# Strassen-style down projection: another order of the seven products, and the residual added in sixteen pieces

## The chip, the cores and the metric

The kernel runs on one core of a Trainium2 chip. The metric is the device time of one execution in microseconds; the time given for a kernel is the median of several runs. The engines are named as the profile names them: PE multiplies matrices (PEld loads its weights), DVE and ACT work on vectors, POOL is used here for some vector work and to issue DMAs that add to what they find, and SP issues the plain DMAs.

## The reference

One decoder layer over 1024 prompt tokens and 64 sample tokens. The change lies in one line of it, the down projection of the gated MLP and the addition to the residual stream, and touches the start of what follows:

```python
def conv_ffn(n, prev, lw):
    a = n @ lw['ffn_w_gate']
    c = n @ lw['ffn_w_up']
    ...
    y = (jax.nn.silu(conv) * c) @ lw['ffn_w_down']        # (1024 x 2816) @ (2816 x 1024)
    ...
    y, conv_new = conv_ffn(rmsnorm(h, lw['g_ffn']), conv_prev, lw)
    h = h + y
    h = h + (p.astype(h.dtype) @ lw['ple_w_proj']) * jax.nn.sigmoid(rmsnorm(h, lw['g_ple']) @ lw['ple_w_gate'])
```

All data are float32. To keep the precision, each operand of a matmul is split into a high and a low part, and three matmuls (high by high, high by low, low by high) stand for one.

## The kernel before

**The stage.** The gated activations have been written to DRAM, one tensor `ds` for each of 22 chunks of 128 of the inner dimension; the residual `h` of the prompt lies in DRAM as `dhp`. The down projection treats the prompt rows as two halves (tiles 0 to 3 and 4 to 7), the 1024 output columns as two halves, and the inner dimension as two halves, and computes the 2x2 block product with seven products of half-size blocks in place of eight. Product numbers 1 to 7 are those of the tuple `SEVEN`. Each product has 11 steps `k`, one for each pair of inner chunks, so there are 77 steps in a fixed order (`steps`). One step on PE is 12 matmuls (`summed`, through `mm3`): four row tiles by three.

**What a step needs.** `load(p, k)` issues two DMAs of 256 KB on SP, four steps ahead in program order (product 5 has a third); they land in one of five buffers called `raw2`. For product 1 they land in `st2`, one buffer for each `k` that stays through the stage and is updated in place by products 5 and 6. `operands(p, k)`, two steps ahead, forms sums or differences with `st2` on DVE (two of 512 columns for products 5 and 6, one of 1024 for product 7, one of 512 for products 4 and 3, none for products 1 and 2), then splits: ACT casts the high part, DVE subtracts to get the low part, both into one of four buffers `o`. So a `raw2` buffer comes free for the next load when DVE has made the low part of its step, and an `o` buffer when PE has done its step. The instruction order on each engine is set by the tile framework's own scheduler, which may place an operation earlier or later than the program text has it; each engine then runs its list in order.

**What a product leaves.** A product's four PSUM accumulators are folded into `h` in SBUF at its last step (`folded(p, t)`, for each row tile `t`): products 1 and 5 by an ACT copy, the others by a DVE addition. Quadrant `h11` is rows 0 to 3 and columns 0 to 511, `h12` the same rows and the other columns, `h21` and `h22` the same for rows 4 to 7. Sums between quadrants that need no accumulator are in `folded_on`, in the steps of the product that follows. `residue(i, j)` adds the residual to a quadrant, by one 1 MB DMA from POOL that accumulates into `h`. Before, the order is 1, 5, 6, 7, 4, 3, 2, so rows 4 to 7 are finished first, by product 4 and the DMA into `h21` after it. In the steps of product 2 stand their normalisation (`normalised`: two ACT squares with a row sum, called `junk`; two small POOL operations, `ss` and `rs`; then `xs`, on DVE or on ACT and POOL) and transposition (`turned`); the scheduler starts the normalisation earlier, in product 3. The last stage (`ple_unit`) takes the rows in the order 4 to 7, then 0 to 3.

Of the kernel before, what the change touches and what calls it, by code (L numbers as in the profile page):

```python
# [13 lines left out]
ALU = mybir.AluOpType  # L14
# [4 lines left out]
P = 128  # L19
D = 1024  # L20
T = 1024
NT = 8
# [7 lines left out]
PLAN = ([0], [], [1, 2, 3])  # L30
VIAP = 20
GS0 = 1
VIAQ = 40
NWB = 10
NF = DFF // P
EPS = 1e-6
# [9 lines left out]
def step_kernel(ctx: ExitStack, tc: tile.TileContext, A):  # L46
    nc = tc.nc
    pe, act, dve, pool, sp = nc.tensor, nc.scalar, nc.vector, nc.gpsimd, nc.sync
# [1311 lines left out]
    cs = cache_stream()  # L1360
# [108 lines left out]
    def xnorm(t, xn, eng):  # L1469
        rows = P if t < NT else R  # L1470
        x = hrows(t)
        r = z["rs"][:rows, t:t + 1]
        if eng is dve:
            dve.scalar_tensor_tensor(xn[:rows], x, r, z["gb"][:rows], ALU.mult, ALU.mult)
# [109 lines left out]
    dhp, dhs = dram.tile([T, D], F32, name="dhp"), dram.tile([R, D], F32, name="dhs")  # L1584
# [290 lines left out]
    NK = NF // 2  # L1875
    opened("hp")
    residual(z["hp"])
    h, hs = z["h"], z["hs"]
# [12 lines left out]
    def xrooms(t):  # L1891

        for e in range(2):
            n = (t + 4) % NT * 2 + e
# [34 lines left out]
    def place_of(k):  # L1929
        return f"st{(k + 3) % NK}"  # L1930

    def load(p, k):
        if p == 1:
            st[k] = z["xs"].tile([P, 2, 512], F32, tag=place_of(k), name="st2", bufs=1)
        r = st[k] if p == 1 else raws()
        a, b = SOURCES[p]
        sp.dma_start(r[:, 0], rows_of(*a, k))
# [26 lines left out]
    def banks(n):  # L1964

        kinds = (pm, pm, p2t, p2t) if n % 2 else (pd, pd, pd, p2)
        return [b([P, 512], "ps_dn") for b in kinds]

    def summed(p, k, t):
        o, tt = opd[p, k], slice(t * P, t * P + P)  # L1970
        mm3(acc[p][t], o[:, 0, 0, tt], o[:, 1, 0, tt], o[:, 0, 1], o[:, 1, 1], k == 0, k == NK - 1)

    def residue(i, j):

        rows, cs = slice(i * 512, i * 512 + 512), slice(j * 512, j * 512 + 512)
        pool.dma_start(h[:, 4 * i:4 * i + 4, cs], dhp[rows, cs].rearrange("(t p) c -> p t c", p=P), accum_op=ALU.add)

    def folded(p, t):

        ps = acc[p][t]  # L1980
        h11, h12, h21, h22 = (h[:, i, j:j + 512] for i in (t, t + 4) for j in (0, 512))
        if p == 1:
            act.copy(h11, ps)
        elif p == 5:
            act.copy(h22, ps)
        elif p == 6:
            dve.tensor_tensor(h12, h11, ps, ALU.add)
        elif p == 7:
            dve.tensor_tensor(h21, h12, ps, ALU.subtract)
        else:  # L1990
            hx = {4: h21, 3: h12, 2: h11}[p]
            dve.tensor_tensor(hx, hx, ps, ALU.add)

    def folded_on(p, t):

        h12, h21, h22 = h[:, t, 512:], h[:, t + 4, 0:512], h[:, t + 4, 512:]
        if p == 7:
            dve.tensor_tensor(h12, h12, h22, ALU.add)
            dve.tensor_tensor(h22, h22, h21, ALU.add)

    def ple_gate(c):
# [41 lines left out]
    for i, (p, k) in enumerate(steps):  # L2043
        if i + 4 < len(steps):
            load(*steps[i + 4])
        if i + 2 < len(steps):
            operands(*steps[i + 2])
        if k == 0:
            acc[p] = banks(i // NK)
        q = SEVEN[i // NK - 1] if i >= NK else 0  # L2050
        if p == 2 and k == NK - 2:
            continue
        for t in range(4):
            for k_ in ((k - 1, k) if p == 2 and k == NK - 1 else (k,)):
                summed(p, k_, t)
            if k == NK - 1:
                folded(p, t)
        if q and 1 <= k <= 4:
            folded_on(q, k - 1)
        for when, quad in (((7, 3), (0, 0)), ((4, 6), (1, 1)), ((4, 7), (0, 1)), ((3, 1), (1, 0))):  # L2060
            if (p, k) == when:
                residue(*quad)
        if p == 1 and k == 1:
            for half in range(2):
                fold_sample(acc_s[half], half)
        elif p == 1 and k == 4:
            xn[NT] = normalised(NT)
        elif p == 1 and k == 7:
            turned(NT, xn[NT])
        elif p == 3 and k == 8:  # L2070
            wpl = ple_gate(0)
        elif p == 2:
            if k in (0, 1, 3, 5):
                t = 4 + (k + 1) // 2
                xn[t] = normalised(t)
            if k in (2, 4, 6, 8):
                t = 3 + k // 2
                turned(t, xn[t])
            if k in (5, 7):
                pT.append(ple_in(k // 7))  # L2080
    for t in range(2):
        xn[t] = normalised(t)


# [17 lines left out]
    def ple_proj(c):  # L2102
        return wload(z["pl"], A["ple_w_proj"][0][:, c * 256:(c + 1) * 256], 2, 256, "wj", 2, st=stg)
# [43 lines left out]
    for c in range(4):  # L2147
        last = c == 3
        nxt = None
        for n, ts in enumerate(((4, 5), (6, 7), None, (0, 1)) + (((2,), (3,)) if last else ((2, 3),))):  # L2150
            if ts:
                ple_unit(c, ts, ws)
            else:
                ple_sample(c, ws)
            if c == 0 and n < 2:
                for t in (2 * n, 2 * n + 1):
# [56 lines left out]
```

## Time and profile before

| | |
|---|---|
| median of 3 runs | 2242.73 us (2241.42 to 2244.2) |
| the profiled execution | 2243.74 us, span 2242.0 us |
| busy in the span | PE 95%, DVE 75%, ACT 61%, POOL 55% |
| first and last start of the stage's matmuls | 1871.7 and 2106.4 us |
| mean granted clock of PE over the span | 0.984 |

Times inside the execution are counted from the start of the span. In a row of the timeline stand the start, the length, the engine, the line and operation, the tile written and read, and in brackets how long the engine was idle before it and what ended that. In a row that groups instructions, three numbers with strokes are the shortest, median and longest duration in ns. In a row by stretches, each engine has its busy time and, in brackets, its instruction count. In the DMA parts, q1 is the queue of SP and q0 that of POOL.

### The profile page before, as it was taken

The page shows a single profiled execution, that of the slowest core. Times are in us where ns is not written, and L with a number is a line of the kernel's source. Part 1 is how long each engine was busy: PE and PEld are TensorE (multiplying, and loading weights), DVE is VectorE, ACT ScalarE, POOL GpSimd, SP SyncE. Part 2 cuts the span into 40 slices and gives each one's busy share as a digit, 9 for nine tenths or more (in the row PEclk, how much of TensorE's full clock was granted, in tenths as well). Part 3 has the DMA queues.
Part 4 walks back from the last instruction along what each step waited for, and adds up shares of the span by engine and source line. Part 5 has one row for each costly group of instructions (what it writes and reads, how often), then busy time and mean ns, then how long its engine had stood idle before and what let it go on. Part 6 is the DMA issues. An engine that isn't in the chain of part 4 may idle for free.

```text
span 2242.0 us, 38332 instructions
## 1 busy us (share of the span) xinstructions
PE 2140.5 (95%) x13459; PEld 1932.5 (86%) x13459; DVE 1674.3 (75%) x2542; ACT 1360.7 (61%) x3692; POOL 1232.3 (55%) x1320
## 2 busy tenths in 40 slices
PE   7999989999999999999999988999999999998999
PEld 6889978878888888887888877999999998876899
DVE  4775766467788888886878888888888877976632
ACT  5576766777778898887777765434333334434521
POOL 5675667576777777776545558665656560002000
PEclk9899999999999999999999998999999999999999
DMA  5343235413242222212422132323232327667321
GB/s 179 108 144 104 82 115 160 130 56 86 85 126 66 60 60 69 63 56 72 138 78 74 55 117 63 108 90 100 89 100 85 104 72 243 228 173 217 99 77 37
DMA packets 204354, 233.59 MB, mean 104 GB/s; under 512 B 42238, under 2 KB 146147, under 8 KB 204163
## 3 DMA queue, kind: packets, MB, share of 16 engines
q1 hardware_dynamic: 188387, 180.01, 25.6%
q0 software_dynamic: 14544, 46.67, 7.2%
q10 hardware_dynamic: 1232, 4.46, 0.5%
q8 instruction: 108, 1.77, 0.3%
q14 instruction: 83, 0.68, 0.1%
HBM read 188.52 MB, written 42.52 MB: 103 GB/s over the span
## 4 chain that ended last, share of the span: by engine, by line
PE 76%; DVE 8%; ACT 5%; DMA 5%; POOL 3%; issue 2%; SPq 0%; ACTq 0%; DVEq 0%; POOLq 0%
PE ps_gu L140 7%; PE ps_gu L141 7%; PE ps_gu L139 7%; PE ks L139 5%; PE ks L141 4%; PE ks L140 4%; PE cpv L645 2%; PE ctp L522 2%; PE ps_dn L140 2%; PE ps_dn L141 2%; PE ps_dn L139 2%; PE ps_pj L139 2%; PE ps_lt L278 2%; PE ps_pj L140 1%; PE ps_pj L141 1%
## 5 line engine op out<-in xcount | busy, mean ns | idle before, releaser
L560 ACT ACTIVATE csq<-ks 128x256 f32<-128x256 f32 x1040 | 392.5, 400 | 86.7 <-PE ks L141 77.6
L565 DVE TENSOR_REDUCE css<-csq 128x16 f32<-128x1024 f32 (+1 forms) x264 | 315.6, 1196 | 64.6 <-ACT csq L560 63.5
L116 ACT CAST wh<-st 128x512 fp32r<-128x512 f32 x176 | 108.3, 619 | 184.9 <-PE ps_gu L140 164.3
L139 PE MATMUL ks<-mv0h,cTh 128*128 128x320 f32 (+1 forms) x520 | 171.5, 332 | 6.5 <-ACT csq L560 2.9
L139 PE MATMUL ks<-mv1h,cTh 128*128 128x320 f32 (+1 forms) x520 | 169.0, 327 | 7.7 <-ACT sn L562 3.6
L604 POOL TENSOR_TENSOR chl<-craw,chl 128x1024 fp32r<-128x1024 f32 x64 | 141.3, 2207 | 57.2 <-ACT chl L603 56.6
L140 PE MATMUL ks<-mv0l,cTh 128*128 128x320 f32 (+1 forms) x520 | 152.7, 295 | 0.0
L140 PE MATMUL ks<-mv1l,cTh 128*128 128x320 f32 (+1 forms) x520 | 152.6, 295 | 0.0
L141 PE MATMUL ks<-mv0h,cTl 128*128 128x320 f32 (+1 forms) x520 | 148.3, 298 | 0.9 <-DVE cTl L117 0.8
L141 PE MATMUL ks<-mv1h,cTl 128*128 128x320 f32 (+1 forms) x520 | 148.2, 299 | 0.1
L630 POOL TENSOR_TENSOR phl<-sn,phl 128x512 fp32r<-128x512 f32 (+1 forms) x64 | 84.9, 1327 | 106.5 <-ACT phl L629 106.0
L117 DVE TENSOR_TENSOR wl<-st,wh 128x512 fp32r<-128x512 f32 x132 | 119.0, 903 | 28.4 <-ACT wh L116 28.4
L140 PE MATMUL ps_dn<-o 128*128 128x512 f32 x308 | 122.9, 399 | 8.8 <-DVE o L117 8.6
L117 POOL TENSOR_TENSOR wl<-st,wh 128x512 fp32r<-128x512 f32 x44 | 69.5, 1581 | 105.0 <-ACT wh L116 105.0
L141 PE MATMUL ps_dn<-o 128*128 128x512 f32 x308 | 121.2, 394 | 0.0
L117 DVE TENSOR_TENSOR cTl<-ctp,cTh 128x512 fp32r<-128x512 f32 (+1 forms) x136 | 90.0, 662 | 38.9 <-ACT cTh L116 38.0
L562 ACT COPY sn<-ks 128x64 f32<-128x64 f32 x520 | 116.6, 224 | 0.0
L139 PEld LDWEIGHTS ks<-mv0h,cTh 128*128 128x128 f32 x520 | 98.6, 190 | 20.6 <-ACT sn L562 7.3
L139 PEld LDWEIGHTS ks<-mv1h,cTh 128*128 128x128 f32 x520 | 98.5, 189 | 19.7 <-ACT sn L562 7.5
L139 PE MATMUL ps_dn<-o 128*128 128x512 f32 x308 | 109.9, 395 | 5.5 <-ACT o L116 5.5
L1317 POOL TENSOR_TENSOR pl<-p,ph 128x512 fp32r<-128x512 f32 (+1 forms) x96 | 97.4, 1019 | 31.3 <-DVE ph L1316 21.3
L141 PE MATMUL ps_gu<-xrh,wl 128*128 128x320 f32 x352 | 108.7, 309 | 0.0
(674 smaller groups left out, 7881.1 us busy)
## 6 DMA issues: line engine op xcount, KB each, us to landing
raw<-ds SPq DMA_DIRECT2D x77, 256.0 KB
raw<-ffn_w_down SPq DMA_DIRECT2D x66, 256.0 KB
stage<-w_in SPq DMA_DIRECT2D x48, 256.0 KB
st<-ffn_w_gate SPq DMA_DIRECT2D x44, 256.0 KB
st<-ffn_w_up SPq DMA_DIRECT2D x44, 256.0 KB
wr<-ffn_w_down SPq DMA_DIRECT2D x44, 256.0 KB
ds<-cv SPq DMA_DIRECT2D x21, 512.0 KB
oraw<-doT SPq DMA_DIRECT2D x16, 256.0 KB
```

Of the source, the lines that this page charges most:

```text
L116: act.copy(hi, src)
L117: (lo_eng or dve).tensor_tensor(lo, src, hi.bitcast(F32), ALU.subtract)
L139: pe.matmul(ps, ah, bh, start=first, stop=False)
L140: pe.matmul(ps, ah, bl, start=False, stop=False)
L141: return pe.matmul(ps, al, bh, start=False, stop=last)
L278: pe.matmul(ps, x, w, start=first, stop=last)
L560: act.activation(sq[:, f * 256:f * 256 + 256], ks[:, 0:256], AF.Square)
L562: act.copy(o.sn[:, g0 + i, :], ks[:, 256:320])
L565: dve.tensor_reduce(o.ss[:, g0 + i + 1 - n:g0 + i + 1, :].rearrange("p i h -> p (i h)"), sq2[:, :n].rearrange("p i (h n) -> p (i h) n", n= ...
L604: pool.tensor_tensor(ch[:, c0:c1, 128:256], src, ch[:, c0:c1, 0:128].bitcast(F32), ALU.subtract)
L630: pool.tensor_tensor(phl[:, :nt, 64:128], sb, phl[:, :nt, 0:64].bitcast(F32), ALU.subtract)
L1317: pool.tensor_tensor(pl[:, c0:], p[:, c0:], ph[:, c0:].bitcast(F32), ALU.subtract)
```

## The change

The order of the products becomes 1, 5, 6, 3, 7, 2, 4. Rows 0 to 3 are now finished first (by product 2), so the normalisation and transposition written in the steps of the last product now take rows 0 to 3 and stand in product 4, and the last stage takes rows 0 to 3 first; the mask `VIAQ` and the rooms for the transposed rows are mirrored with it. Product 5 is copied to `h22` and also to `h12` (four more ACT copies), product 6 goes into `h21`, and `h12` gets it through `folded_on`. The number of DVE additions is the same, 28. They are written at steps 1, 3, 5 and 7 of the following product, where they stood at steps 1 to 4. The residual comes by row tile: sixteen DMAs of 256 KB, each written two steps after the one before, the quadrants in the order 22, 11, 12, 21 in the steps of products 6, 3, 7 and 2.

```diff
-    SEVEN = (1, 5, 6, 7, 4, 3, 2)
+    SEVEN = (1, 5, 6, 3, 7, 2, 4)
...
-    def residue(i, j):
-        rows, cs = slice(i * 512, i * 512 + 512), slice(j * 512, j * 512 + 512)
-        pool.dma_start(h[:, 4 * i:4 * i + 4, cs], dhp[rows, cs].rearrange("(t p) c -> p t c", p=P), accum_op=ALU.add)
+    def residue(i, j, t):
+        rows, cs = slice((4 * i + t) * P, (4 * i + t + 1) * P), slice(j * 512, j * 512 + 512)
+        pool.dma_start(h[:, 4 * i + t, cs], dhp[rows, cs], accum_op=ALU.add)
...
         elif p == 5:
             act.copy(h22, ps)
+            act.copy(h12, ps)
         elif p == 6:
-            dve.tensor_tensor(h12, h11, ps, ALU.add)
+            dve.tensor_tensor(h21, h11, ps, ALU.add)
         elif p == 7:
-            dve.tensor_tensor(h21, h12, ps, ALU.subtract)
+            dve.tensor_tensor(h21, h21, ps, ALU.subtract)
         else:
-            hx = {4: h21, 3: h12, 2: h11}[p]
+            hx = {3: h12, 2: h11, 4: h21}[p]
             dve.tensor_tensor(hx, hx, ps, ALU.add)
...
-        if p == 7:
-            dve.tensor_tensor(h12, h12, h22, ALU.add)
+        if p == 6:
+            dve.tensor_tensor(h12, h12, h21, ALU.add)
+        elif p == 7:
             dve.tensor_tensor(h22, h22, h21, ALU.add)
...
-        if q and 1 <= k <= 4:
-            folded_on(q, k - 1)
-        for when, quad in (((7, 3), (0, 0)), ((4, 6), (1, 1)), ((4, 7), (0, 1)), ((3, 1), (1, 0))):
-            if (p, k) == when:
-                residue(*quad)
+        if q and k in (1, 3, 5, 7):
+            folded_on(q, k // 2)
+        for p0, k0, i_, j_ in ((6, 2, 1, 1), (3, 3, 0, 0), (7, 3, 0, 1), (2, 3, 1, 0)):
+            if p == p0 and k >= k0 and (k - k0) % 2 == 0 and k - k0 < 8:
+                residue(i_, j_, (k - k0) // 2)
...
-        elif p == 2:
+        elif p == 4:
             if k in (0, 1, 3, 5):
-                t = 4 + (k + 1) // 2
+                t = (k + 1) // 2
                 xn[t] = normalised(t)
```

What the scheduler makes of it is seen at three places.

ACT, where the normalisation of the first finished rows meets the casts of the operands. Before, this is in product 3: the first row casts its step 5, the cast after the first `junk` its step 6.

```order
L116 CAST o_25503<-raw2_25460 128x1024
L1465 ACTIVATE junk_25695,ss_24233<-h_24231 128x512
L116 CAST o_25522<-raw2_25480 128x1024
L1465 ACTIVATE junk_25697,ss_24233<-h_24231 128x512
L1465 ACTIVATE junk_25721,ss_24233<-h_24231 128x512
L1465 ACTIVATE junk_25723,ss_24233<-h_24231 128x512
L116 CAST o_25541<-raw2_25499 128x1024
L1465 ACTIVATE junk_25782,ss_24233<-h_24231 128x512
L1476 ACTIVATE xs_25727<-h_24231,rs_24234 128x1024
```

After, it is in product 4; the first row casts step 2, the cast after two `junk` step 3.

```order
L116 CAST o_25684<-raw2_25637 128x1024
L1465 ACTIVATE junk_25703,ss_24233<-h_24231 128x512
L1465 ACTIVATE junk_25705,ss_24233<-h_24231 128x512
L116 CAST o_25715<-raw2_25657 128x1024
L1465 ACTIVATE junk_25730,ss_24233<-h_24231 128x512
L1465 ACTIVATE junk_25732,ss_24233<-h_24231 128x512
L1465 ACTIVATE junk_25793,ss_24233<-h_24231 128x512
L116 CAST o_25743<-raw2_25680 128x1024
L1465 ACTIVATE junk_25795,ss_24233<-h_24231 128x512
L1476 ACTIVATE xs_25736<-h_24231,rs_24234 128x1024
```

Before, the first square reads a row tile of `h21`, which the last 1 MB DMA writes. After, it reads `h11`, which DVE has just finished with product 2; the DMAs into `h11` and `h12` belong to products 3 and 7.

DVE, after a product that is followed by sums between quadrants. Before, this is product 4, steps 2 and 3 (`o` is the low part of the operands, L1957 forms the operands of a later step, L1989 folds product 7, L1998 and L1999 are the sums without an accumulator):

```order
L1989 TENSOR_TENSOR h_24231<-h_24231,ps_dn_25000 128x512
L1998 TENSOR_TENSOR h_24231<-h_24231 128x512
L1989 TENSOR_TENSOR h_24231<-h_24231,ps_dn_25001 128x512
L1957 TENSOR_TENSOR raw2_25254<-raw2_25254,st2_24323 128x512
L1989 TENSOR_TENSOR h_24231<-h_24231,ps_dn_25002 128x512
L1998 TENSOR_TENSOR h_24231<-h_24231 128x512
L117 TENSOR_TENSOR o_25237<-raw2_25187,o_25237 128x1024
L1999 TENSOR_TENSOR h_24231<-h_24231 128x512
L1998 TENSOR_TENSOR h_24231<-h_24231 128x512
L1957 TENSOR_TENSOR raw2_25275<-raw2_25275,st2_24341 128x512
L1998 TENSOR_TENSOR h_24231<-h_24231 128x512
L1999 TENSOR_TENSOR h_24231<-h_24231 128x512
```

After, the same product 7 is followed by product 2 (L1990 folds product 7, L2001 is the sum that follows):

```order
L1990 TENSOR_TENSOR h_24231<-h_24231,ps_dn_25232 128x512
L117 TENSOR_TENSOR o_25447<-raw2_25403,o_25447 128x1024
L1990 TENSOR_TENSOR h_24231<-h_24231,ps_dn_25233 128x512
L2001 TENSOR_TENSOR h_24231<-h_24231 128x512
L1990 TENSOR_TENSOR h_24231<-h_24231,ps_dn_25234 128x512
L1990 TENSOR_TENSOR h_24231<-h_24231,ps_dn_25235 128x512
L2001 TENSOR_TENSOR h_24231<-h_24231 128x512
L117 TENSOR_TENSOR o_25469<-raw2_25422,o_25469 128x1024
L2001 TENSOR_TENSOR h_24231<-h_24231 128x512 x2
L117 TENSOR_TENSOR o_25488<-raw2_25444,o_25488 128x1024
```

Four sums fewer stand between the splits, and no operand is formed there. The sums are not at every other step, as the text has them, but close together again.

DVE, early in product 6. Before, the low part of step 3 (`o_24795`) comes right after the last operands of product 6:

```order
L1952 TENSOR_TENSOR st2_24403<-raw2_24890,st2_24403 128x512
L117 TENSOR_TENSOR o_24795<-st2_24264,o_24795 128x1024
L1955 TENSOR_TENSOR raw2_24910<-raw2_24910,st2_24255 128x1024
L117 TENSOR_TENSOR o_24815<-st2_24275,o_24815 128x1024
L1955 TENSOR_TENSOR raw2_24930<-raw2_24930,st2_24258 128x1024
L117 TENSOR_TENSOR o_24835<-st2_24297,o_24835 128x1024
```

After, the operands of the first two steps of product 3 stand ahead of that low part (`o_24799`):

```order
L1952 TENSOR_TENSOR st2_24403<-raw2_24896,st2_24403 128x512
L1959 TENSOR_TENSOR raw2_24917<-raw2_24917,st2_24255 128x512
L1959 TENSOR_TENSOR raw2_24937<-raw2_24937,st2_24258 128x512
L117 TENSOR_TENSOR o_24799<-st2_24264,o_24799 128x1024
L117 TENSOR_TENSOR o_24819<-st2_24275,o_24819 128x1024
L117 TENSOR_TENSOR o_24840<-st2_24297,o_24840 128x1024
```

Two loads of product 3 must now have landed before that low part is made.

On POOL the sixteen DMAs stand where the four stood, in one piece, ahead of the small operations of the normalisation. By what each waits for, the first four (`h22`) can go as soon as ACT has copied product 5, the next four (`h11`) as DVE folds product 6, the next (`h12`) as DVE folds product 3, and the last (`h21`) as DVE makes the sums of L2001.

More of the change, by code (lines that the diff above doesn't have):

```diff
@@ L32 @@
 GS0 = 1
-VIAQ = 40
+VIAQ = 130
 NWB = 10
@@ L1893, in xrooms @@
         for e in range(2):
-            n = (t + 4) % NT * 2 + e
+            n = t * 2 + e
             if n < NK:
@@ L2050, in step_kernel @@
         q = SEVEN[i // NK - 1] if i >= NK else 0
-        if p == 2 and k == NK - 2:
+        if p == 4 and k == NK - 2:
             continue
         for t in range(4):
-            for k_ in ((k - 1, k) if p == 2 and k == NK - 1 else (k,)):
+            for k_ in ((k - 1, k) if p == 4 and k == NK - 1 else (k,)):
                 summed(p, k_, t)
@@ L2069, in step_kernel @@
             turned(NT, xn[NT])
-        elif p == 3 and k == 8:
+        elif p == 2 and k == 8:
             wpl = ple_gate(0)
-        elif p == 2:
+        elif p == 4:
             if k in (0, 1, 3, 5):
-                t = 4 + (k + 1) // 2
+                t = (k + 1) // 2
                 xn[t] = normalised(t)
             if k in (2, 4, 6, 8):
-                t = 3 + k // 2
+                t = k // 2 - 1
                 turned(t, xn[t])
@@ L2080, in step_kernel @@
                 pT.append(ple_in(k // 7))
-    for t in range(2):
+    for t in (4, 5):
         xn[t] = normalised(t)
@@ L2149, in step_kernel @@
         nxt = None
-        for n, ts in enumerate(((4, 5), (6, 7), None, (0, 1)) + (((2,), (3,)) if last else ((2, 3),))):
+        for n, ts in enumerate(((0, 1), (2, 3), None, (4, 5)) + (((6,), (7,)) if last else ((6, 7),))):
             if ts:
@@ L2155, in step_kernel @@
             if c == 0 and n < 2:
-                for t in (2 * n, 2 * n + 1):
+                for t in (4 + 2 * n, 5 + 2 * n):
                     turned(t, xn[t])
```

## The prediction

> **What bounds the kernel now.** The page first: PE is the busiest engine by far, so time is won where PE waits.
>
> ```profile
> span 2242.0 us, 38332 instructions
> PE 2140.5 (95%) x13459; PEld 1932.5 (86%) x13459; DVE 1674.3 (75%) x2542; ACT 1360.7 (61%) x3692; POOL 1232.3 (55%) x1320
> ```
>
> Second, PE's timeline gives its pace with everything ready. Two starts of the same matmul, one step of 12 apart, are 2.72 us apart: 0.227 us each, 29.9 us for a product of 11 steps.
>
> ```profile
> 2046.35 0.39 PE L139 MATMUL ps_dn<-o 128*128 128x512 f32 x1
> 2049.07 0.39 PE L139 MATMUL ps_dn<-o 128*128 128x512 f32 x1
> ```
>
> Third, the stage cut at its products, all instructions counted. The rows are products 7, 4, 3 and 2; the columns are the stretch, its length, the engines' busy times, the granted clock, the DMA share and GB/s.
>
> ```profile
> 1965.00:1996.00 31.00, 29.62 (x129) 23.71 (x128) 20.43 (x21) 10.78 (x11) 1.41 (x1) 1.00 0.68 186
> 1996.00:2032.00 36.00, 31.73 (x134) 24.38 (x132) 25.74 (x33) 10.88 (x11) 2.56 (x2) 1.00 0.79 215
> 2032.00:2073.00 41.00, 34.01 (x132) 26.02 (x132) 25.67 (x28) 18.00 (x29) 13.81 (x10) 0.92 0.63 183
> 2073.00:2106.80 33.80, 33.80 (x165) 27.98 (x164) 20.62 (x25) 15.41 (x26) 1.27 (x4) 1.00 0.28 96
> ```
>
> Less 29.9 us each, the losses are 1.1, 6.1 and 11.1 us: 18.3 in three products. Product 2 has some 31 transposes among its matmuls, which account for its 3.9 us, and PE was never idle there. So 18.3 us is all that the change can win in this stretch.
>
> Fourth, who makes PE wait: the waits of PE, the four residual DMAs on POOL, and ACT and PE after the last of them.
>
> ```profile
> PE ps_dn L140 <- DVE o L117: 8.1, 8, 1.7
> PE ps_dn L139 <- ACT o L116: 4.4, 1, 4.4
> ...
> 1968.37 1.41 POOL L1976 DMA_DIRECT2D h<-dhp  x1 [91.68 <-DMA raw<-ffn_w_down]
> 2009.24 1.29 POOL L1976 DMA_DIRECT2D h<-dhp  x1 [39.47 <-DVE h L1998]
> 2013.31 1.28 POOL L1976 DMA_DIRECT2D h<-dhp  x1 [2.78 <-DVE h L1999]
> 2040.74 1.28 POOL L1976 DMA_DIRECT2D h<-dhp  x1 [26.16 <-DVE h L1992]
> ...
> 2052.56 0.63 ACT L1465 ACTIVATE junk<-h 128x512 bf16<-128x512 f32 x1 [12.86 <-DMA h<-dhp]
> 2053.19 1.03 ACT L116 CAST o<-raw 128x1024 fp32r<-128x1024 f32 x1
> ...
> 2054.27 0.80 PE L139 MATMUL ps_dn<-o 128*128 128x512 f32 x1 [4.36 <-ACT o L116]
> 2065.09 0.49 PE L140 MATMUL ps_dn<-o 128*128 128x512 f32 x1 [1.51 <-DVE o L117]
> ```
>
> ACT ran into a square that needs the last residual DMA and stood 12.86 us, with the casts of the operands queued behind it; PE used up what was prepared and stopped. That is product 3. Product 4 is another matter: two 1 MB DMAs within 4 us, and the loads of the operands beside them. The chain of waits shows a load at its usual 3.0 us (1996.27), and the same kind of load beside the residual:
>
> ```profile
> 1971.63 9.19 DMA raw<-ffn_w_down
> 1996.27 3.01 DMA raw<-ffn_w_down
> 2014.78 11.94 DMA raw<-ds
> 2040.74 11.73 DMA h<-dhp
> ```
>
> DVE's timeline says why a late load stops PE: operands of a later step stand ahead of a split that PE needs sooner, and DVE runs in order.
>
> ```profile
> 1980.93 1.23 DVE L1955 TENSOR_TENSOR raw<-raw,st 128x1024 f32<-128x1024 f32 x1 [2.05 <-DMA raw<-ffn_w_down]
> 1982.08 1.22 DVE L117 TENSOR_TENSOR o<-raw,o 128x1024 fp32r<-128x1024 f32 x1
> 2019.86 0.69 DVE L1957 TENSOR_TENSOR raw<-raw,st 128x512 f32<-128x512 f32 x1 [3.97 <-DMA raw<-ffn_w_down]
> 2020.47 1.22 DVE L117 TENSOR_TENSOR o<-raw,o 128x1024 fp32r<-128x1024 f32 x1
> ```
>
> **The change, part by part.**
>
> *The wait on the last residual goes.* In the new order the squares that start early read `h11` and `h12`. Their residual belongs to the end of products 6 and 3, a product or more earlier. The last residual (`h21`) is read again only by the fold of product 4, at the stage's end. Product 3's 11.1 us are this wait: the idle 4.36 us, the matmuls after it at half pace (granted clock 0.92 over the stretch), the idle 1.51 us, and small ones. I take back all 11.1.
>
> *The normalisation now meets product 4.* Its casts have no DMA to wait for, but DVE still forms operands there, where product 2 had none: 11 of 0.69 us, and 1.22 us of split each, 21 us of DVE in 30, beside the rows below.
>
> ```profile
> L1465 ACT ACTIVATE junk<-h x32: 617/631/637, 1310.2 to 2108.5; 128x512 bf16<-128x512 f32 x32
> L1474 DVE SCALAR_TENSOR_TENSOR xs<-h,rs,gb x6: 1272/1284/1285, 2056.9 to 2124.8; 128x1024 f32<-128x1024 f32 x6
> L1985 ACT COPY h<-ps_dn x4: 588/600/621, 1933.8 to 1935.3; 128x512 f32<-128x512 f32 x4
> ```
>
> In the new list the first `xs` stands on DVE ahead of the split of step 3. Its chain from the fold is two squares (1.3 us), the two POOL operations and `xs` itself (1.3). The POOL pair:
>
> ```profile
> 2056.91 1.91 POOL L1466 TENSOR_SCALAR ss<-ss 128x1 f32<-128x1 f32 x1
> 2058.91 1.39 POOL L1467 TENSOR_TENSOR rs<-ss,mhalf 128x1 f32<-128x1 f32 x1
> ```
>
> That is up to 3.4 us more, 6 in all. When product 2 ends, three steps are split ahead, 8.2 us of PE, so the split of step 3, 1.2 us after `xs`, comes in time. I take 1 us of loss, with 0 and 6 as ends: the 6 is one whole chain in the open.
>
> *The residual as four groups.* What each waits for sets when it goes. `h11` goes as product 6 is folded, as before (1968.4, now a few us sooner and by row tile). Before, this group cost product 7 1.1 us; now product 3 stands there, with an operand of 0.69 us in place of 1.22. I keep 1. `h12` goes as product 3 is folded, alone, in product 7. Before, this place (product 4) had 2 MB and twelve folds and sums; now there are 1 MB and four folds. Its price lies between 1.1, one group with splits three steps ahead, and 6.1, two groups and the sums; the splits will not be fully ahead, since a load is tied to the split two places before it, and product 7 has the long operands. I take 3. `h21` goes in product 2, which forms no operands on DVE, so that a late load stops no split but its own, and five buffers of loads lie ahead. I take 0.5, ends 0 and 1.1.
>
> `h22` goes at the end of product 5, about 1935 to 1940. There the queues are full until 1943.5 and then empty for 14 us:
>
> ```profile
> DMA  9997897898892899930000000000000000000006
> GB/s 346 366 382 276 271 365 192 322 358 276 292 339 85 295 290 333 336 137 5 0 0 0 0 0 0 0 0 0 0 0 0 22 0 0 0 0 0 0 0 216
> ```
>
> (1930 to 1960 in 40 parts.) The megabyte is pushed into the empty part. The DMA's own work is no larger than before: 26.0% of 25 us, 6.5 us of all 16 engines, for 1.05 MB.
>
> ```profile
> q1 hardware_dynamic: 2008, 3.65, 44.7%
> q0 software_dynamic: 528, 1.05, 26.0%
> ```
>
> (1960 to 1985; packets, MB, share.) What may hurt is DVE's list: two operands of product 3 now stand ahead of the split of step 3 of product 6. The rows of the same places before, SP's loads and the split:
>
> ```profile
> 1932.25 0.33 SPq L1937 DMA_DIRECT2D raw<-ds  x1
> 1933.46 0.33 SPq L1937 DMA_DIRECT2D raw<-ds  x1
> ...
> 1939.83 1.22 DVE L117 TENSOR_TENSOR o<-st,o 128x1024 fp32r<-128x1024 f32 x1
> ```
>
> The pair's loads are issued before the residual. The split ended at 1941.05, and PE needed it eight steps before product 6 ended at 1965, at 1943.2: 2.2 us to spare. Two operands of 0.69 us in front of it use 1.4 of them. I take 0.5 us of loss, ends 0 and 4 (the pair's loads some 4 us late).
>
> *The copies and the sums.* Four ACT copies of 0.60 us are 2.4 us at the end of product 5, where ACT waits for PE between casts (26.1 of 55 us busy) and DVE is the one that is late; nothing, and up to 1 us without that cover. Sixteen issues in place of four: each took 1.28 to 1.41 us on POOL, whole megabytes; sixteen are at most 23 us over 100, on an engine that is otherwise idle there. Nothing. The twelve folds and sums that stood together become eight and eight; their gain is within the 3 us of product 7. The last stage does the same work in the mirrored order of rows: nothing, within 1 us.
>
> ```profile
> 1905.00:1960.00 55.00, 55.00 (x245) 45.53 (x244) 50.77 (x63) 26.14 (x29) 0.00 (x0) 1.00 0.67 229
> ```
>
> **The sum.** Losses before 18.3. After: 0.5 (product 6), 1 (product 3), 3 (product 7), 0.5 (product 2), 1 (product 4), together 6. The gain is 12.3 us. The profiled execution took 2243.74 us, 1.7 more than its span and 1.0 more than the median of the runs; against the median of 2242.73 the gain leaves 2230.4.
>
> **The rivals.**
>
> *A: the lead is not rebuilt, and the change is slower.* The place is product 4: three chains of normalisation stand on DVE ahead of splits. If product 2 ends with nothing split ahead, each chain is open: 3 times 6 us is 18. With product 7 at its full 6.1 and 1.5 in products 6 and 3, that is 25.6, 7 more than now: 2250. It decides at some 5 us of PE idle a chain. For it: DVE has 21 us of operands and splits in this product. Against: product 2 has only splits on DVE, 13 of 30 us with some folds, so it can run ahead as far as the four `o` buffers allow. 0.07.
>
> *B: bursts decide, not the wait.* Each group of 1 MB stops DVE as 2 MB did before, 6.1 us in products 3, 7 and 2 of the new order, since the scheduler has put each group into one piece: with 0.5 and 1 that is 19.8, and the time is 2244, no change. For it: loads took 9.2 and 11.9 us beside a residual. Against: the first group before cost only 1.1. 0.06.
>
> *C: a fixed price for each DMA.* A plain load of 256 KB took 3.0 us; if the sixteen do the same one after the other, a group holds the queues 12 us, where 1 MB took 11.7. That is no loss by these rows, but if a group also keeps the loads back for its four completions (3.0 each on top of 11.7), three groups in operand-forming products each cost 3 to 4 us more: 2241. 0.04. The Trainium skill, DMA: Bandwidth & Descriptors, section on the anatomy of one DMA, gives about 2.0 us for each DMA plus its bytes at 436 GB/s; by this rule sixteen of them take an estimated 24 us more than four, against the change. The trace does not agree on the time of a megabyte (11.7 us, where the rule has 4.4), and the landing is nobody's wait in the new order.
>
> *D: nothing is left.* Groups spread over row tiles cost nothing, only product 4's 1 us: 2225. 0.15.
>
> **How the numbers follow.** The forecast, 2230 with its own range of 2226 to 2237, has 0.68. D has 0.15, B and C 0.10, A 0.07. A measurement of this kernel tells 0.2%, 4.5 us, from no change. Faster by that: the forecast, D and a little of C, 0.84; same, 0.08; slower 0.08. The range for 8 in 10 takes in D's 2225 and reaches to 2239, where product 7 and product 4 both take their upper ends.
>
> **What would show it.** ACT's squares should have no wait on `h<-dhp`; product 4 in the old list, now product 7, should lose about 3 us; PE's clock should be 1.00 in every product; four clusters of POOL issues near 1935, 1965, 1997 and 2028. It is wrong if PE waits on DVE in the last product by more than 6 us, or if the split of step 3 of product 6 comes late.

## The result, and the profile after

The changed kernel took 2228.22 us (median of 4 runs, 2226.04 to 2231.13), the kernel before 2242.53 beside it (4 runs, 2241.42 to 2244.2): ratio 0.9936, 95% interval 0.9919 to 0.9954, which is 14.3 us saved where 12.3 were forecast. Run again in a later session (e8 below), where the kernel before took 2245.59, it gave 0.9925 (0.9912 to 0.9938). The kernel before itself took 2242.5 to 2246.7 us in the different sessions, so below only ratios to the kernel before of the same session, or lengths inside a trace, are compared.

The page after the change, its span and engines:

```profile
span 2224.2 us, 38364 instructions
PE 2135.0 (96%) x13459; PEld 1932.2 (87%) x13459; DVE 1672.1 (75%) x2542; ACT 1361.3 (61%) x3696; POOL 1236.5 (56%) x1332
```

The work is the same; PE is busy 5.5 us less; 4.1 of that are old product 3's matmuls, partly at half pace (34.01 us busy of a usual 29.9). The stage cut at its products (6, 3, 7, 2 and 4; columns as in the prediction):

```profile
1932.40:1962.60 30.20, 30.20 (x135) 25.01 (x134) 23.54 (x28) 15.37 (x19) 4.47 (x5) 1.00 0.57 158
1962.60:1992.50 29.90, 29.90 (x134) 24.75 (x133) 23.93 (x27) 11.61 (x11) 2.62 (x3) 1.00 0.71 210
1992.50:2024.90 32.40, 30.99 (x134) 24.68 (x133) 24.99 (x25) 11.57 (x11) 3.48 (x4) 1.00 0.77 226
2024.90:2054.80 29.90, 29.90 (x133) 24.76 (x133) 19.01 (x22) 11.61 (x11) 3.48 (x4) 1.00 0.75 213
2054.80:2088.50 33.70, 33.34 (x159) 27.08 (x158) 26.88 (x31) 21.00 (x41) 11.91 (x13) 1.00 0.29 94
```

Products 6, 3 and 2 have no idle PE at all; the granted clock is 1.00 throughout. Product 7 takes 2.5 us more than 29.9, and product 4 has 25 transposes among its matmuls. What PE still waits for, from 1930 to 2090 us, is shown as the total, the number of times and the longest (1.8 us in all, 12.5 before):

```profile
PE ps_dn L140 <- DVE o L117: 1.4, 3, 0.7
PE pt L132 <- DVE xg L117: 0.4, 1, 0.4
```

The residual DMAs on POOL's timeline:

```profile
1933.27 3.80 POOL L1976 DMA_DIRECT2D h<-dhp  x4 [59.61 <-DMA raw<-ds]
1961.70 0.86 POOL L1976 DMA_DIRECT2D h<-dhp  x1 [24.63 <-DVE h L1988]
...
1995.46 0.86 POOL L1976 DMA_DIRECT2D h<-dhp  x1 [28.48 <-DVE h L1993]
1997.19 1.75 POOL L1976 DMA_DIRECT2D h<-dhp  x2 [0.87 <-DVE h L1993]
1999.52 0.86 POOL L1976 DMA_DIRECT2D h<-dhp  x1 [0.57 <-DVE h L1993]
2026.21 0.86 POOL L1976 DMA_DIRECT2D h<-dhp  x1 [25.83 <-DVE h L2001]
```

Each of the last three groups starts with the first row tile that is ready and follows the others (1995.46 to 1999.52 in the group of `h12`), where a 1 MB DMA had to wait for the fourth. ACT's first square no longer waits for a DMA, only for the fold, and nothing runs short behind it:

```profile
2056.73 0.63 ACT L1465 ACTIVATE junk<-h 128x512 bf16<-128x512 f32 x1 [3.50 <-DVE h L1993]
```

What is left of the old trouble is product 7, where 1 MB still lies among the loads (DVE, then PE):

```profile
2002.30 1.23 DVE L1955 TENSOR_TENSOR raw<-raw,st 128x1024 f32<-128x1024 f32 x1 [1.93 <-DMA raw<-ffn_w_down]
...
2008.09 1.23 DVE L1955 TENSOR_TENSOR raw<-raw,st 128x1024 f32<-128x1024 f32 x1 [2.29 <-DMA raw<-ffn_w_down]
```

```profile
2004.71 0.50 PE L140 MATMUL ps_dn<-o 128*128 128x512 f32 x1 [0.75 <-DVE o L117]
2010.50 0.50 PE L140 MATMUL ps_dn<-o 128*128 128x512 f32 x1 [0.28 <-DVE o L117]
2013.90 0.50 PE L140 MATMUL ps_dn<-o 128*128 128x512 f32 x1 [0.38 <-DVE o L117]
```

### The profile page after: what moved, and what is told of

Same layout as the page of the kernel before. It is cut to its first block, busy times and chain, and to the rows that moved or that the text cites. A ratio compares the mean times of both kernels' runs of the same rounds, so it can differ in the third digit from the quotient of the medians.

```text
span 2224.2 us, 38364 instructions
## 1 busy us (share of the span) xinstructions
PE 2135.0 (96%) x13459; PEld 1932.2 (87%) x13459; DVE 1672.1 (75%) x2542; ACT 1361.3 (61%) x3696; POOL 1236.5 (56%) x1332
## 4 chain that ended last, share of the span: by engine, by line
PE 74%; DVE 9%; DMA 5%; ACT 5%; POOL 4%; issue 3%; SPq 0%; DVEq 0%; POOLq 0%; ACTq 0%
PE ps_gu L140 7%; PE ps_gu L141 7%; PE ps_gu L139 7%; PE ks L139 5%; PE ks L141 4%; PE ks L140 4%; PE cpv L645 2%; PE ctp L522 2%; PE ps_dn L140 2%; PE ps_dn L141 2%; PE ps_dn L139 2%; PE ps_lt L278 2%; PE ps_pj L139 2%; PE ps_pj L140 1%; PE ps_pj L141 1%
## 5 line engine op out<-in xcount | busy, mean ns | idle before, releaser
L139 PE MATMUL ps_gu<-xrh,wh 128*128 128x320 f32 x352 | 108.6, 309 | 0.9 <-ACT xrh L116 0.9
```

Source lines behind the costliest of these rows:

```text
L139: pe.matmul(ps, ah, bh, start=first, stop=False)
```

## The experiments

The measure used throughout is the time from the first matmul of a product to the first of the next, less 29.92 us (11 steps of 2.72); for the last product it ends at the start of its last matmul. Every trace has all 924 matmuls of the stage, 132 for each product, so the products are told apart by counting. The stretches in the prediction's table were cut about 1 us into product 7 and read 1.1, 6.1 and 11.1 us for the old products 7, 4 and 3; by count these lost 2.1, 5.9 and 11.4. The sum from the start of product 5 to the end stands beside the single products. Product 1 is left out: it lost 2.5 to 4.2 us from profile to profile, whatever the kernel (the last section says why). Each row is one profiled execution, and only the ratios carry an interval.

| kernel | order | residual | loss by product, us | last product | products 5 to the last | ratio to before (95%) |
|---|---|---|---|---|---|---|
| before | old | 4 x 1 MB | 6: 0.0; 7: 2.1; 4: 5.9; 3: 11.4 | 3.3 | 202.3 | 1 |
| after | new | 16 x 256 KB | 6: 0.0; 3: 0.0; 7: 2.3; 2: 0.0 | 3.5 | 185.4 | 0.9936 (0.9919 to 0.9954) |
| e1 | new | 4 x 1 MB | 3: 0.8; 7: 6.5; 2: 0.0 | 5.2 | 192.1 | 0.9963 (0.9949 to 0.9977) |
| e2 | old | 16 x 256 KB | 7: 1.0; 4: 5.8; 3: 6.9 | 3.3 | 196.5 | 0.9969 (0.9955 to 0.9983) |
| e11 | new | 16 x 256 KB, late | 3: 0.6; 7: 7.4; 2: 0.0 | 5.2 | 192.6 | 0.9950 (0.9936 to 0.9965) |
| e12 | new | 8 x 512 KB | 3: 0.0; 7: 3.6; 2: 0.0 | 4.2 | 187.3 | 0.9943 (0.9928 to 0.9958) |
| e3 | old | 4 x 1 MB, `h21` first | 7: 1.6; 4: 6.3; 3: 5.0 | 3.3 | 195.8 | 0.9970 (0.9957 to 0.9982) |
| e4 | old | none | 7: 0.0; 4: 0.3; 3: 2.2 | 3.3 | 185.4 | 0.9929 (0.9908 to 0.9950) |
| e5 | new | none | 3: 0.0; 7: 0.0; 2: 0.0 | 2.7 | 182.3 | 0.9915 (0.9900 to 0.9929) |
| e6 | new | 16, `h12` with `h22` | 3: 0.0; 7: 0.4; 2: 0.0 | 3.5 | 183.4 | 0.9920 (0.9906 to 0.9935) |
| e7 | new | 16, `h22` with `h21` | 3: 0.0; 7: 2.4; 2: 1.4 | 6.3 | 189.6 | 0.9942 (0.9927 to 0.9958) |

**The two parts alone.** e1 keeps the new order and adds the residual by four DMAs of 1 MB, each behind the last row tile:

```diff
-    def residue(i, j, t):
+    def residue(i, j):
...
-        rows, cs = slice((4 * i + t) * P, (4 * i + t + 1) * P), slice(j * 512, j * 512 + 512)
-        pool.dma_start(h[:, 4 * i + t, cs], dhp[rows, cs], accum_op=ALU.add)
+        rows, cs = slice(i * 512, i * 512 + 512), slice(j * 512, j * 512 + 512)
+        pool.dma_start(h[:, 4 * i:4 * i + 4, cs], dhp[rows, cs].rearrange("(t p) c -> p t c", p=P), accum_op=ALU.add)
...
-            if p == p0 and k >= k0 and (k - k0) % 2 == 0 and k - k0 < 8:
-                residue(i_, j_, (k - k0) // 2)
+            if p == p0 and k == k0 + 6:
+                residue(i_, j_)
```

> The new order of products, with the residual of each quadrant in one DMA of 1 MB again. Theory (the order of the products removes ACT's wait, the size of the DMAs matters little): within 2 us of the changed kernel, 2228 to 2231 us, no wait of ACT's squares on the residual, product 7 loses 2 to 4 us. Rival (the sixteen small DMAs do it, by not holding the queues for a megabyte): product 7 loses 5 us or more and product 3 too, 2234 us or more.

e2 is the opposite, the old order with sixteen small ones:

```diff
-    def residue(i, j):
+    def residue(i, j, t):
...
-        rows, cs = slice(i * 512, i * 512 + 512), slice(j * 512, j * 512 + 512)
-        pool.dma_start(h[:, 4 * i:4 * i + 4, cs], dhp[rows, cs].rearrange("(t p) c -> p t c", p=P), accum_op=ALU.add)
+        rows, cs = slice((4 * i + t) * P, (4 * i + t + 1) * P), slice(j * 512, j * 512 + 512)
+        pool.dma_start(h[:, 4 * i + t, cs], dhp[rows, cs], accum_op=ALU.add)
...
-                residue(*quad)
+                for t in range(4):
+                    residue(*quad, t)
```

> The old order of products, with the residual by row tile in sixteen DMAs at the old places. Theory (order): ACT still runs into the residual of h21, but now waits for one tile of 256 KB and not for four, some 3 us at first and less behind it; product 3 loses 3 to 5 us in place of 11, product 4 its 6 us as before: 2234 to 2237 us. Rival (small DMAs do it all): 2230 us or less. Rival (order does it all, the size is nothing): 2242 us, ACT's wait near 12 us again.

From product 5 to the end the order alone saves 10.2 us (202.3 to 192.1), the small DMAs alone 5.7 (196.5), both 16.9: nearly the sum. In e2 the wait that the forecast called product 3's is still there, 8.87 us in place of 12.86 (ACT's timeline) where some 3 were expected, and PE's waits from 1930 to 2110 us went from 12.5 to 8.3. The old-order runs differ from the kernel before in more than their DMAs: by the traces, the scheduler also put the first squares two casts earlier on ACT in e2, and three casts earlier in e3 and e4 below, with the first `xs` earlier on DVE, so what they say of single products is rough.

```profile
2045.66 0.63 ACT L1465 ACTIVATE junk<-h 128x512 bf16<-128x512 f32 x1 [8.87 <-DMA h<-dhp]
```

```profile
PE ps_dn L140 <- DVE o L117: 7.9, 9, 1.7
PE ps_dn L139 <- ACT o L116: 0.4, 1, 0.4
```

In e1 product 7 loses 6.5 us, and the theory that the number of DMAs matters little fell. PE, POOL, SP's queue and DVE of e1 around the `h12` residual:

```profile
2003.51 0.50 PE L140 MATMUL ps_dn<-o 128*128 128x512 f32 x1 [0.81 <-DVE o L117]
...
2005.54 1.28 POOL L1976 DMA_DIRECT2D h<-dhp  x1 [35.26 <-DVE h L1993]
...
2007.92 1.17 SPq L1938 DMA_DIRECT2D raw<-ffn_w_down  x1
...
2015.63 1.23 DVE L1955 TENSOR_TENSOR raw<-raw,st 128x1024 f32<-128x1024 f32 x1 [4.70 <-DMA raw<-ffn_w_down]
...
2018.04 0.79 PE L140 MATMUL ps_dn<-o 128*128 128x512 f32 x1 [2.70 <-DVE o L117]
```

**Size, or the late start?** A 1 MB DMA is not only large, it also goes after the last fold: 9.1 us behind the first matmul of product 7 (1996.4), the changed kernel's first piece 3.0 us behind it (1992.5). e11 cuts a quadrant into four DMAs of 256 KB by partitions, so that each waits for all four folds:

```diff
-        rows, cs = slice((4 * i + t) * P, (4 * i + t + 1) * P), slice(j * 512, j * 512 + 512)
-        pool.dma_start(h[:, 4 * i + t, cs], dhp[rows, cs], accum_op=ALU.add)
+        rows, cs, ps = slice(i * 512, i * 512 + 512), slice(j * 512, j * 512 + 512), slice(32 * t, 32 * t + 32)
+        pool.dma_start(h[ps, 4 * i:4 * i + 4, cs], dhp[rows, cs].rearrange("(t p) c -> p t c", p=P)[ps], accum_op=ALU.add)
...
-            if p == p0 and k >= k0 and (k - k0) % 2 == 0 and k - k0 < 8:
-                residue(i_, j_, (k - k0) // 2)
+            if p == p0 and k == k0 + 6:
+                for t in range(4):
+                    residue(i_, j_, t)
```

> Four DMAs of 256 KB for a quadrant as in the changed kernel, but cut by partitions (32 partitions, all four row tiles), so that each waits for the last of the four folds, as a 1 MB DMA does, and the four then go back to back. Theory that the late start of a 1 MB DMA is what costs (it goes only after the last fold): product 7 loses 5 to 6 us and product 3 about 1, as with 1 MB DMAs (6.1 and 1.2), and the time is 4 to 5 us over the changed kernel's, ratio to the kernel before 0.9950 to 0.9965. Theory that the size of one DMA costs (it keeps the loads behind it for longer): product 7 loses 2 to 2.5 us, as with small ones, and the ratio is 0.992 to 0.9935. Not separated from this: a DMA on 32 partitions may go slower than one on 128; then the landings are over 10 us and the loss is above 6.

e12 goes halfway, two DMAs of 512 KB (row tiles 0 and 1, then 2 and 3):

```diff
-        rows, cs = slice((4 * i + t) * P, (4 * i + t + 1) * P), slice(j * 512, j * 512 + 512)
-        pool.dma_start(h[:, 4 * i + t, cs], dhp[rows, cs], accum_op=ALU.add)
+        rows, cs = slice((4 * i + t - 1) * P, (4 * i + t + 1) * P), slice(j * 512, j * 512 + 512)
+        pool.dma_start(h[:, 4 * i + t - 1:4 * i + t + 1, cs], dhp[rows, cs].rearrange("(t p) c -> p t c", p=P), accum_op=ALU.add)
...
-            if p == p0 and k >= k0 and (k - k0) % 2 == 0 and k - k0 < 8:
+            if p == p0 and k - k0 in (2, 6):
```

> Two DMAs of 512 KB for a quadrant, row tiles 0 and 1 and then 2 and 3, in the changed kernel's order. If the cost follows the start after the folds or the size, product 7 lies about midway between 2.3 (four DMAs) and 6.1 (one): 4 us, product 3 about 0.5, and the ratio to the kernel before is 0.994 to 0.996. If the cost comes only with the last fold's wait, half of the bytes go early and the other half late: 3 us.

e10 wrote the four row tiles from the last to the first, to delay the first of them:

```diff
-                residue(i_, j_, (k - k0) // 2)
+                residue(i_, j_, 3 - (k - k0) // 2)
```

In it the last row tile of `h22` takes up `h21` with its residual already added.

> Each group's four small DMAs are written from the last row tile to the first, so the first of them waits for the last of the four folds, as the 1 MB DMA does, and then the four go back to back. Theory that the time of the start decides (a group that starts at the first fold and follows the folds is through before the loads pile up): product 7 loses 5 to 6 us, as with the 1 MB DMAs (6.1), product 3 about 1, and the stage is 3 to 5 us longer than the changed kernel's: ratio 0.9950 to 0.9960. Theory that the size decides (a small DMA lets a load past between two of them, a large one holds it): product 7 loses 2 to 2.5 us as in the changed kernel, and the time is the same within 1 us.

e10 tells nothing apart: POOL's first issue in product 7 came 3.4 us behind its first matmul, where the changed kernel's came 3.0 behind, so the delay was not obtained. Product 7 lost 2.7 us, the ratio was 0.9930 (0.9915 to 0.9945). e11 does tell: small DMAs that start late cost as much as one large one (7.4 against 6.5 us in product 7, 192.6 against 192.1 in all), both starting 9.1 us behind the first matmul. POOL, DVE and PE of e11:

```profile
2005.46 3.54 POOL L1976 DMA_DIRECT2D h<-dhp  x4 [32.75 <-DVE h L1993]
...
2016.08 1.23 DVE L1955 TENSOR_TENSOR raw<-raw,st 128x1024 f32<-128x1024 f32 x1 [5.24 <-DMA raw<-ffn_w_down]
...
2018.50 0.50 PE L140 MATMUL ps_dn<-o 128*128 128x512 f32 x1 [3.19 <-DVE o L117]
```

Product 7 of e12, with its first piece 5.5 us behind the first matmul, lost 3.6:

```profile
2000.98 1.20 POOL L1976 DMA_DIRECT2D h<-dhp  x1 [30.91 <-DVE h L1993]
2003.31 1.20 POOL L1976 DMA_DIRECT2D h<-dhp  x1 [1.13 <-DVE h L1993]
```

So size by itself is not the cause; what it costs goes with the delay of the group. By the first piece's start after the first matmul, the loss of product 7 goes 2.7 us: 1.7 (e8, the changed kernel again); 3.0: 2.3; 3.2: 2.4 (e7); 3.4: 2.7 (e10); 5.5: 3.6 (e12); 9.1: 6.5 (e1) and 7.4 (e11). Three things go into the last two, and these runs do not fully part them. One is the group's own start. Another is the lead that DVE brought into product 7, which was smaller in e1 and e11, since their `h11` group had been late too: product 3 lost 0.8 and 0.6, and PE waited 0.81 and 0.76 us for DVE before the `h12` residual was issued (in e1 at 2003.51). The third is a stretch at half clock behind their longest stop, worth an estimated 1.5 and 1.7 us (last section). Less these two, e1 lost some 4 and e11 some 5 us, against 3.6 in e12 and 2.3 in the changed kernel. e11's DMAs also used a little more of the DMA engines, 28.6% of 25 us against 25.0% in e1.

**What the old order lost.** e3 keeps the old order and the 1 MB DMAs, and only exchanges which quadrant comes when, `h21` first, so that ACT's squares find theirs done:

```diff
-        for when, quad in (((7, 3), (0, 0)), ((4, 6), (1, 1)), ((4, 7), (0, 1)), ((3, 1), (1, 0))):
+        for when, quad in (((7, 3), (0, 0)), ((4, 6), (1, 0)), ((4, 7), (1, 1)), ((3, 1), (0, 1))):
```

> The old order and four DMAs of 1 MB, but the residual of h21 is added in product 4, ahead of h22 and h12, so that it has landed before the squares read it. Theory: ACT's wait is gone and product 3 loses under 3 us where it lost 11; all of 3 MB now lie in product 4, which loses 8 to 11 us in place of 6: 2234 to 2238 us. Rival (the wait of ACT was a symptom, PE was short of loads anyway): product 3 still loses 8 us or more, 2242 us or more.

e4 leaves the residual out altogether (`h` lacks it from there on), in the old order:

```diff
-        for when, quad in (((7, 3), (0, 0)), ((4, 6), (1, 1)), ((4, 7), (0, 1)), ((3, 1), (1, 0))):
-            if (p, k) == when:
-                residue(*quad)
```

> The old order with the residual left out altogether (so h lacks it). It splits what product 4 lost between the DMAs and the cluster of folds and sums on DVE. Theory: product 7 loses nothing, product 4 loses 2 to 3 us to the cluster, product 3 under 1 us: 2226 to 2229 us, about the changed kernel's time. Rival (the cluster of sums is the larger part of product 4's loss): product 4 loses 5 us, 2230 us or more.

e5 leaves it out in the new order, by the same cut:

> The changed kernel with the residual left out altogether (so h lacks it): the floor for any placing of it. Theory: of the four groups only that of h12 costs anything, in product 7, where 2.5 us of idle PE go down to under 0.7: 2225.5 to 2226.5 us. Rival (the groups cost PE in other places too, or slow DVE and PE by traffic): 2224 us or less. Rival (product 7 loses by its long operands, not by the residual): product 7 still loses 2 us, 2228 us.

PE's waits from 1930 to 2110 us in e3 and in e4:

```profile
PE ps_dn L140 <- DVE o L117: 9.8, 9, 2.0
```

```profile
PE ps_dn L140 <- DVE o L117: 1.5, 1, 1.5
```

ACT's wait is gone in e3 and product 3 falls from 11.4 to 5.0 us, not under the 3 expected: there PE waits for splits on DVE, and 2.2 us are left without any residual (e4, where under 1 was expected). Some 3 of the 6.4 us that went are the half clock that followed the old stop of 4.36 us (5.74 us of matmuls at half pace, last section). Product 4 of e3, with 3 MB in it, lost 6.3 us and not the 8 to 11 expected. Without the residual product 4's 5.9 become 0.3, with its twelve folds and sums in one place all the same. So those sums cost next to nothing, and of the old 19.4 us in products 7, 4 and 3 the residual DMAs made 16.9: some 6 by ACT's wait and what followed it, the rest beside the loads. In the new order without the residual products 6, 3, 7 and 2 lose nothing; 185.4 less 182.3 is 3.1 us, all that the sixteen DMAs still cost, 2.3 of it in product 7 and 0.8 in product 4, where e5's forecast had product 7 alone.

**Where to put them.** e6 sends `h12` (product 5's copy is all that it needs) right behind `h22` into the empty queues of product 6, e7 the opposite, `h22` beside `h21` into product 2, which forms no operands:

```diff
-        for p0, k0, i_, j_ in ((6, 2, 1, 1), (3, 3, 0, 0), (7, 3, 0, 1), (2, 3, 1, 0)):
+        for p0, k0, i_, j_ in ((6, 2, 1, 1), (3, 3, 0, 0), (6, 3, 0, 1), (2, 3, 1, 0)):   # e6
+        for p0, k0, i_, j_ in ((3, 3, 0, 0), (7, 3, 0, 1), (2, 3, 1, 1), (2, 3, 1, 0)):   # e7
```

> The changed kernel, with the residual of h12 added right behind that of h22, at the end of product 5, where the queues were empty for 14 us before: 2 MB there, none in product 7. Theory: product 7 loses under 0.7 us, products 6 and 3 lose nothing as DVE's list there has the time: 2226 us, 2 us less than the changed kernel. Rival (the empty stretch is not long enough for 2 MB and the loads; the operands of product 3 stand ahead of the splits of product 6 on DVE): products 6 and 3 lose 3 us or more, 2229 us or more.

> The changed kernel, with the residual of h22 added beside that of h21, in product 2: 2 MB in one burst in a product that forms no operands on DVE. Theory (a burst costs PE where late loads stop splits of nearer steps on DVE): product 2 loses under 1.5 us, 2228 to 2230 us. Rival (a burst of 2 MB costs by the time it holds the queues, as in product 4 before): product 2 loses 4 us or more, 2232 us or more.

Product 7 of e6 loses 0.4 in place of 2.3, and e6 stands 1.1 us above the kernel without any residual (183.4 and 182.3). In its trace e7 refutes that a burst is free where no operand is formed: its eight DMAs at 2028.45 cost product 2 1.4 us, and product 4, where DVE came with less lead, lost 6.3 against 3.5. Its ratio to the kernel before does not tell it from the changed kernel's. POOL and DVE of e7:

```profile
2028.45 7.12 POOL L1976 DMA_DIRECT2D h<-dhp  x8 [25.62 <-DVE h L2001]
...
2049.70 0.69 DVE L1957 TENSOR_TENSOR raw<-raw,st 128x512 f32<-128x512 f32 x1 [6.62 <-DMA raw<-ffn_w_down]
```

The last two runs put the changed kernel and e6 on one chip:

> The changed kernel once more, beside the two below on one chip, so that they can be compared directly. Both theories expect 0.993 to 0.994 of the kernel before, and in the trace the losses over 29.9 us a product seen so far: 2.3 us in product 7, none in 3 and 2.

> The residual of h12 right behind that of h22, once more, now beside the changed kernel. If the 2.3 us that product 7 lost is the residual DMAs among its loads, product 7 loses 0.4 us again and the time is 1.5 to 2 us below the changed kernel's, 0.9991 to 0.9993 of it. If the earlier difference was one between chips, the two are equal within 0.5 us.

Medians 2230.07 (5 runs) and 2226.59 (6 runs), ratios to the kernel before 0.9925 (0.9912 to 0.9938) and 0.9923 (0.9906 to 0.9941): by whole runs the two cannot be told apart. In the traces product 7 loses 1.7 and 0.2 us, and products 5 to the last take 185.6 and 183.2, 2.4 us apart, as against 2.0 in the pair before. PE's waits from 1930 us on, in e8 and then in e9, and e9's POOL:

```profile
PE ps_dn L140 <- DVE o L117: 1.2, 3, 0.5
PE pt L132 <- DVE xg L117: 0.3, 1, 0.3
```

```profile
PE pt L132 <- DVE xg L117: 0.3, 1, 0.3
...
1935.38 7.22 POOL L1976 DMA_DIRECT2D h<-dhp  x8 [59.63 <-DVE o L117]
```

## Why the prediction was right, and where it was not

*The bound and the sign* held. By count the three old products had lost 19.4 us in place of 18.3; the middle three now (3, 7 and 2) lose 2.3, so 17.1 came back.

*The wait on the last residual* went as said, but the 11.1 us put down to it were two things. e3 shows some 6 us as ACT's wait; 5.0 stay when it is gone, 2.2 of them even without a residual. Taking all 11.1 back was right only because the change also took that place's other waits for loads away. For that part the prediction gave no reason, so there it was lucky.

*The groups* were the mis-sized terms. Product 3 was given 1 us and lost 0.0; product 7 was given 3 and lost 2.3; product 2 was given 0.5 and lost 0.0. They were priced from the old whole megabytes; e1 shows what those cost in the new order, 0.8, 6.5 and, in products 2 and 4, 0.0 and 1.7 more than now. The prediction noted of `h11` that it goes sooner by row tile, but gave this no price; it missed the gain, that a cut group starts with the first fold. Its 3 for product 7 was picked between 1.1 and 6.1, and that it came near is in part luck.

*`h22` in the empty part* was given 0.5 and lost nothing: the two operands stood ahead of the splits as the instruction list had it, and PE never waited in product 6. The split of step 3, the first of the three below, ended at 1940.79, 0.9 us before the first matmul that reads it; the prediction's 2.2 us to spare less 1.4 gave 0.8. DVE's rows there, and that matmul:

```profile
1938.38 1.28 DVE L1959 TENSOR_TENSOR raw<-raw,st 128x512 f32<-128x512 f32 x2
1939.58 3.49 DVE L117 TENSOR_TENSOR o<-st,o 128x1024 fp32r<-128x1024 f32 x3
...
1941.70 0.39 PE L140 MATMUL ps_dn<-o 128*128 128x512 f32 x1
```

*Product 4's chains of normalisation* were given 1 us. Product 4 lost 3.5 us, 2.7 of which e5 has too, where the 25 transposes stand with no idle PE; the other 0.8 (PE idle for 0.36, and what follows it) comes with the residual, since e5 has the same chains. So the size was near and the cause another: the chains alone cost nothing. The after-sum of 6 is thus 3.1, and the gain by this account 16.3. The two traces differ by 16.9 from product 5 on, as the new last product has 25 transposes in it where the old has 29 (2.7 us and 3.3 us with no idle PE), and by 15.3 with product 1, which lost 1.6 more in the new trace by its own scatter. The measured 14.3 has an interval of 10 to 18. Both errors of the forecast, 18.3 for 19.4 and 6 for 3.1, made it too small.

*The sums written further apart* had nothing to win: the scheduler put them close together again, and e4 prices the old cluster at 0.3 us at most.

*The rivals.* A: no chain stood open. B, at 6.1 us for each group, is what product 7 does with late groups (e1, e11), not products 3 and 2, and not with groups that follow the folds. C: the DMA engines' share shows no price for each DMA. Over 25 us that hold one quadrant, in after (from 1995 us):

```profile
q1 hardware_dynamic: 2330, 4.24, 51.4%
q0 software_dynamic: 576, 1.05, 25.8%
```

The old megabyte took 26.0%. The Trainium skill, DMA: Bandwidth & Descriptors, section on bandwidth, has the rule to batch DMAs to at least 1 MiB for 75% of the peak rate or more; followed here it would have cost time, since the sixteen use no more of the engines and win 6.7 us over the four (192.1 to 185.4). D, that nothing is left, was right for three groups of four in their own products; e6 brings the fourth within 0.4.

*The signs it named* came: ACT's squares waited for no DMA, product 7 lost 2.3 us of some 3, PE's clock was 1.00 in every product from 6 on, and POOL's groups began at 1933, 1962, 1995 and 2026 us.

## What to carry to other kernels

Cut a DMA that accumulates into a finished operand at the granularity at which that operand is finished: it then starts with the first piece, and what it saves is the delay, not bytes. Put such DMAs where the load queue is empty (e6), not merely where the engine beside it has less to do (e7), since a lead lost in one product is paid in the next; this rests on the traces, as whole runs do not tell e6 or e7 from the changed kernel. When one wait is blamed for a loss, exchange the order of what it waits for and look at what remains: here 5 of 11 us did.

## What was not expected of the hardware

An accumulated byte took about twice the time of the DMA engines that a loaded one took. Over 1931 to 1957 us of the changed kernel 3.06 MB of loads took 35.6% of the 16 engines, 1.05 MB of residual 23.5%: 11.6 against 22.4% for a megabyte.

```profile
q1 hardware_dynamic: 2132, 3.06, 35.6%
q0 software_dynamic: 576, 1.05, 23.5%
```

A stop of PE can cost more than its length, and the length does not decide whether it does. In e1 the stop of 2.70 us is followed by half clock, 3.41 us of it, in e11 one of 3.19 us, in e2 one of only 1.67 us; in e12 one of 2.64 us is followed by none. At half clock the matmuls come 0.43 us apart in place of 0.227, so such a stretch costs an estimated 1.5 to 1.7 us. The changes of the granted clock in one trace lie whole multiples of 3.41 us apart, and each of these stretches begins at the end of such an interval. In this stage PE was idle for 48% or more of the interval ahead of every new stretch. Intervals with at most 46% were followed by none. Near half it is open: the 51% of e12 were followed by none. So a stop counts by how it falls into the intervals. The interval with the stop and the one behind it, in e1, e2 and e12, then the kernel before, where the stop of 4.36 us filled one interval and 6.83 us at half clock followed:

```profile
2014.18:2017.59 3.41, 1.17 (x6) 0.62 (x4) 1.96 (x2) 0.58 (x1) 0.00 (x0) 1.00 1.01 368
2017.59:2021.00 3.41, 2.96 (x7) 2.38 (x8) 3.41 (x4) 1.51 (x2) 0.00 (x0) 0.50 0.48 157
...
2051.27:2054.68 3.41, 1.73 (x7) 0.89 (x6) 2.20 (x3) 3.41 (x7) 1.95 (x3) 1.00 0.64 235
2054.68:2058.09 3.41, 3.41 (x9) 2.67 (x8) 2.94 (x2) 3.18 (x5) 3.32 (x3) 0.50 0.48 154
...
2010.52:2013.93 3.41, 1.67 (x8) 1.05 (x6) 1.51 (x2) 0.14 (x1) 0.00 (x0) 1.00 0.92 329
2013.93:2017.35 3.42, 2.52 (x11) 2.07 (x12) 3.42 (x4) 1.97 (x2) 0.00 (x0) 1.00 0.46 144
...
2050.23:2053.64 3.41, 0.00 (x0) 0.00 (x0) 0.00 (x0) 1.08 (x3) 0.00 (x0) 1.00 0.97 311
2053.64:2060.47 6.83, 5.74 (x13) 4.18 (x14) 4.85 (x5) 4.35 (x11) 5.09 (x4) 0.50 0.24 77
```

This is also product 1's scatter. Ahead of and at its start PE stops for 1.23 and 1.16 us in every profile; the nine profiles in which half clock followed lost 3.5 to 4.2 us there, the other five 2.5 to 2.6.

The Trainium skill, TensorE: Matmul & The Clock Gate, Part 1, has a free-running window of about 3.4 us: an array idle for a window runs at half rate until a busy window has passed. The intervals and their length agree (3.41 us); but a whole idle window was not needed, since windows with 48 to 66% of idle PE were enough (e1, e2, e11).
